# Loading the weights of an FFN layer's first two groups by pairs of tiles, and earlier

## The chip, the cores and the metric

The kernel runs on one core of one Trainium2 chip. The metric is the time of one execution in device microseconds, the median of the runs. A profile is one execution, recorded by the hardware profiler; its times are microseconds from the first instruction (the span's start). TensorE (PE in the profile; PEld for its weight loads) multiplies, VectorE (DVE), ScalarE (ACT) and GpSimd (POOL) work element by element, SyncE (SP) issues most DMA transfers.

## The reference

A two-layer decoder trunk over 512 positions of 1024 channels in float32. Each layer adds a mixer to the residual stream and then a gated FFN:

```python
hn = rms_norm(h, norm_ffn[layer])
g  = causal_dwconv3(hn @ w_gate, conv_w) + conv_b      # 1024 -> 2816
up = hn @ w_up                                         # 1024 -> 2816
h  = h + (jax.nn.silu(g) * up) @ w_down                # 2816 -> 1024
```

`rms_norm` divides by the root of the mean square over the 1024 channels and multiplies by a gain. After layer 1 a final `rms_norm` is applied. The two mixers (gated convolution with pooling in layer 0, spatial gating in layer 1) are not touched by the change.

## The kernel before

**Precision.** Every float32 product is made of three matmuls: an operand is split into a rounded high part and the remainder (`hi` and `lo`), and `mm3` (L135 to L137) adds hi·hi, hi·lo and lo·hi in one PSUM bank. Splitting a weight tile is `parts` (L130, L131): ScalarE rounds `raw` to `whi`, VectorE subtracts to get `wlo`. A matmul of 128x128 weights with 512 positions is one of the 128x512 rows.

**Layout.** The residual stream is held transposed: eight tiles `h[k]` of 128 channels by 512 positions. `hg[k]` holds the split of `h[k]` times the norm's gain. The list `PAIRS` is 0, 4, 1, 5, 2, 6, 3, 7: the order in which the eight channel tiles are multiplied. A "step" below is one entry of `PAIRS`, counted from 0.

**The FFN.** `Ffn.hidden(f)` produces two of the 22 hidden tiles, f and f+1, from a group of weights: 256 columns of the gate and 256 of the up matrix, each loaded in two tiles ("halves") of four channel tiles, 512 KB each. Group f = 0 is multiplied by `direct` before the norm's factor is known, on `hg` with the gain only; the factor `rstd` is applied to the outputs when they leave PSUM (`evacuate`). In step order, each step makes twelve matmuls: two gate and two up outputs, three each. Inside this group two short pieces of TensorE work find the factor: `rstd_tokens` (L211, L212: sums of squares over channels, into columns, with the last tile's square kept apart in `last`), then a short chain on VectorE and ScalarE, then `rstd_spread` (L219: the columns turned into a full tile, copied by ScalarE, L222). Then `normalize(kp)`, four times, makes the normalized `hg` of tiles kp and kp+4 (`x` at L560, the split at L564 and L565) and sums and differences of halves of them (`t`, L572 to L575; L580 to L582 split these, where the low part is made by a copy of the negative and a DMA on GpSimd's queue that adds `t` to it). Group f = 2 is multiplied by `direct` on the normalized tiles, first the gate outputs (48 matmuls), then the up outputs (48). All later groups go through `seven`, which needs the sums too and starts with the `ua` product (L649).

In layer 1, `sums` puts the split of the sums into the buffers of `h[kp]` and `h[kp+4]`, which are free once the residual has been turned: `turn_residual` (L872, four transposes; L874, ScalarE's copy) brings `h` back to positions by channels, half a row of 128 positions each time, eight times in all. Before, one turn stands ahead of each of the eight steps of group 0.

**Buffers.** Weight tiles rotate: four `raw`, five `whi`, five `wlo`. `x` and `t` share three buffers with the tag "sum". TensorE has seven PSUM banks with the tag "mm" and one apart.

**Order of the work.** The engines run their own queues in order. The order within a queue is chosen when the program is built, from the order in which the source issues the operations and from when their inputs and buffers are expected. In the program before, VectorE's `wlo` of group 2's second gate half comes, in layer 0, after all but the last operation of the normalizing, and in layer 1 about half way; the up halves of that group come later still.

Of the kernel before, what the change touches and what calls it, by code (L numbers as in the profile page):

```python
# [8 lines left out]
F32 = mybir.dt.float32  # L9
# [6 lines left out]
P = 128  # L16
# [14 lines left out]
def tile_trunk(ctx: ExitStack, tc: tile.TileContext, x, norm_mix, norm_ffn, final_norm,  # L31
# [3 lines left out]
    nc = tc.nc  # L35
# [4 lines left out]
    wp = ctx.enter_context(tc.tile_pool(name="wp", bufs=1))  # L40
# [86 lines left out]
    def parts(raw, a, b, name):  # L127
        hi = wp.tile([P, a, b], F32R, tag="whi", bufs=5, name=f"whi_{name}")
        lo = wp.tile([P, a, b], F32R, tag="wlo", bufs=5, name=f"wlo_{name}")
        nc.scalar.activation(hi, raw, AF.Copy)  # L130
        nc.vector.tensor_tensor(lo, raw, hi.bitcast(F32), ALU.subtract)  # L131
        return hi, lo

    def mm3(ps, lhs, rhs, start, stop):
        nc.tensor.matmul(ps, lhs[0], rhs[0], start=start, stop=False)  # L135
        nc.tensor.matmul(ps, lhs[0], rhs[1], start=False, stop=False)  # L136
        nc.tensor.matmul(ps, lhs[1], rhs[0], start=False, stop=stop)  # L137
# [27 lines left out]
    def hg_k(k):  # L165
        return hg[k][0], hg[k][1]
# [313 lines left out]
    def ffn_weights(layer, f, order):  # L480
        cs = slice(f * P, (f + 2) * P)
        return {(key, half): fetch(
            (w_ffn_gate if key == "g" else w_ffn_up)[layer][half * 512 : (half + 1) * 512, cs]
            .rearrange("(k p) c -> p k c", p=P), 4, 256, f"{key}{layer}_{f}_{half}")
            for key, half in order}

    class Ffn:
# [27 lines left out]
        def act(self, ft, s):  # L515
            self.acts[ft] = split(self.ap, s, f"a{self.layer}_{ft}", tag="a", bufs=6)

        def direct(self, f, normed, sets, before=lambda i: None):

            layer = self.layer  # L520
            order = [(key, half) for js in sets for half in range(2)
                     for key in dict.fromkeys("gu"[j // 2] for j in js)]
            ch = {key: parts(*raw) for key, raw in ffn_weights(layer, f, order).items()}
            banks = {}
            for js in sets:
                for i, k in enumerate(PAIRS):
                    before(i)
                    for j in js:
                        hi, lo = ch["gu"[j // 2], k // 4]
                        c = slice((j % 2) * P, (j % 2 + 1) * P)  # L530
                        if j not in banks:
                            banks[j] = mm_bank(f"gu{layer}_{f}_{j}")
                        mm3(banks[j], (hi[:, k % 4, c], lo[:, k % 4, c]), hg_k(k),
                            i == 0, i == NK - 1)

            def evacuate():
                r = self.r
                gates = []
                for j in range(2):
                    t = padded_tile()  # L540
                    if normed:
                        nc.scalar.copy(t[:, 2:], banks[j])
                    else:
                        nc.vector.tensor_tensor(t[:, 2:], banks[j], r, ALU.mult)
                    s = self.silu(self.conv(t, f + j), f + j)
                    if not normed:
                        nc.gpsimd.tensor_tensor(s, s, r, ALU.mult)
                    gates.append(s)
                for j, s in enumerate(gates):
                    nc.vector.tensor_tensor(s, banks[2 + j], s, ALU.mult)  # L550
                    self.act(f + j, s)

            return evacuate
# [140 lines left out]
            nc.vector.tensor_tensor(s0, kept[:, :2, :], s0, ALU.mult)  # L694
            self.act(f, s[0])

        def hidden(self, f, before=lambda i: None):
            if f == 0:
                def first(i):
                    before(i)  # L700
                    if i == 2:
                        self.norm.rstd_tokens()
                    elif i == 4:
                        self.r = self.norm.rstd_spread()

                rest = self.direct(0, False, (range(4),), first)
                for kp in range(NP - 1):
                    self.normalize(kp)
                rest()
                self.normalize(NP - 1)  # L710
            elif f == 2:
                self.direct(2, True, ((0, 1), (2, 3)))()
            else:
                self.seven(f)

# [142 lines left out]
    def ffn1(norm):  # L858
        with tc.tile_pool(name="f1", bufs=1) as ap:
            def sums(kp):  # L860
                return [cp.tile([P, 2, HALF], F32R, tag=f"h{k}", name=f"t23_{k}")
                        for k in (kp, kp + NP)]

            ffn = Ffn(1, prm1, norm, ap, sums)
            acts = ffn.acts
            y = [ap.tile([P, D], F32, name=f"y{t}") for t in range(NT)]
            ssf = ap.tile([P, NT, PAD], F32, name="ssf")[:, :, :2]

            def turn_residual(t, half):
                ps = mm_bank(f"hT{t}_{half}")  # L870
                for i in range(4):
                    nc.tensor.transpose(ps[:, i * P : (i + 1) * P],  # L872
                                        h[half * 4 + i][:, t * P : (t + 1) * P], ident)
                nc.scalar.copy(y[t][:, half * 512 : (half + 1) * 512], ps)  # L874

            def before(k):
                if k < 4:
                    turn_residual(k, 0)
                elif k < 8:
                    turn_residual(k - 4, 1)  # L880

            for a, b in PARTS:
                for f in range(a, b, 2):
                    ffn.hidden(f, before=before)
                last = b == NF
                if last:
                    fin = wp.tile([P, D], F32, tag="raw", bufs=4, name="fin")
                    nc.scalar.dma_start(
                        fin, final_norm.rearrange("(o d) -> o d", o=1).to_broadcast([P, D]))
                    root = small[:, 2:3]  # L890
                    nc.scalar.activation(root, eps, AF.Sqrt)
                ch = {}
                for ft in range(a, b):
                    ch[ft] = weights(w_ffn_down[1][ft * P : (ft + 1) * P, :]
                                     .rearrange("(k p) c -> p k c", p=P), 1, D, f"dn1_{ft}")

                def lhs(ft, j):
                    ts_ = slice((j // 2) * P, (j // 2 + 1) * P)
                    return acts[ft][0][:, ts_], acts[ft][1][:, ts_]

                def rhs(ft, j):
                    c = slice((j % 2) * 512, (j % 2 + 1) * 512)
                    return ch[ft][0][:, 0, c], ch[ft][1][:, 0, c]

                yf = {}

                def done(j, ps):
                    t, half = j // 2, j % 2
                    dst = y[t][:, half * 512 : (half + 1) * 512]
                    nc.vector.tensor_tensor(dst, ps, dst, ALU.add)  # L910
                    if not last:
                        return
                    sq = tp.tile([P, S], F32, tag="sq", name=f"sqf{j}")
                    ss = ssf[:, t, half : half + 1]
                    nc.scalar.activation(sq, dst, AF.Square, accum_out=ss)
                    yf[half] = ap.tile([P, S], F32, tag="s", bufs=3, name=f"yf{j}")
                    nc.vector.tensor_tensor(yf[half], dst, fin[:, half * 512 : (half + 1) * 512],
                                            ALU.mult)
                    if half == 0:
                        nc.vector.tensor_scalar(ss, ss, 1.0 / D, EPS, op0=ALU.mult, op1=ALU.add)  # L920
                        return
                    ms = ssf[:, t, 0:1]
                    nc.vector.scalar_tensor_tensor(ms, ss, 1.0 / D, ms, op0=ALU.mult, op1=ALU.add)
                    r = tp.tile([P, LINE], F32, tag="rc", name=f"rc_fin{t}")[:, :1]
                    newton(ms, 1, f"fin{t}", r)
                    nc.vector.tensor_scalar(ms, ms, 1.5, None, op0=ALU.add)
                    for c in range(2):
                        cs = slice(c * 512, (c + 1) * 512)
                        nc.vector.tensor_scalar(y[t][:, cs], yf[c], r, ms,
                                                op0=ALU.mult, op1=ALU.mult)  # L930
                        nc.sync.dma_start(out[t * P : (t + 1) * P, cs], y[t][:, cs])

                group8(f"dn{a}", list(range(a, b)), lhs, rhs, 4, done)
# [47 lines left out]
```

## Time and profile before

| | |
|---|---|
| median of 3 runs | 1031.02 us (1030.04 to 2592.89) |
| profiled execution, its own time | 1031.83 us |
| its span, first to last instruction | 1029.8 us |
| mean granted TensorE clock | 0.991 of full speed |
| TensorE busy | 1004.6 us, 5169 matmuls |
| VectorE, ScalarE, GpSimd busy | 609.5, 471.6, 93.8 us |
| HBM read | 98.42 MB, 98 GB/s over the span |

A row of the order in time has start, duration, engine, line, operation, output<-inputs, sizes and count, and in brackets the idle time of that engine before it with what ended it. A row of waits has engine, output and line, what it waited for, then the total in us, the number of times, and the longest. Matmuls overlap: a row of 0.39 us is followed by the next start 0.23 us later. The granted clock is the share of full speed that TensorE was allowed. A table row by stretches has the stretch, its length, busy time of TensorE, its weight loads, VectorE, ScalarE and GpSimd with numbers of instructions, then the granted clock, the DMA share and GB/s.

### The profile page before, as it was taken

The page shows a single profiled execution, that of the slowest core. Times are in us where ns is not written, and L with a number is a line of the kernel's source. Part 1 is how long each engine was busy: PE and PEld are TensorE (multiplying, and loading weights), DVE is VectorE, ACT ScalarE, POOL GpSimd, SP SyncE. Part 2 cuts the span into 40 slices and gives each one's busy share as a digit, 9 for nine tenths or more (in the row PEclk, how much of TensorE's full clock was granted, in tenths as well). Part 3 has the DMA queues.
Part 4 walks back from the last instruction along what each step waited for, and adds up shares of the span by engine and source line. Part 5 has one row for each costly group of instructions (what it writes and reads, how often), then busy time and mean ns, then how long its engine had stood idle before and what let it go on. Part 6 is the DMA issues. An engine that isn't in the chain of part 4 may idle for free.

```text
span 1029.8 us, 12982 instructions
## 1 busy us (share of the span) xinstructions
PE 1004.6 (98%) x5169; PEld 856.7 (83%) x5169; DVE 609.5 (59%) x878; ACT 471.6 (46%) x689; POOL 93.8 (9%) x105
## 2 busy tenths in 40 slices
PE   9999998899999999999999999989999999999996
PEld 6788886788998899889888888867889988998885
DVE  5997556755556455736843645377645564664566
ACT  5423435551644246326555443476424532660553
POOL 3141122200000000000310001122000000000000
PEclk9999999899999999999999999999999999999998
DMA  7432233442454243524343123245415342543432
GB/s 228 155 102 82 82 115 69 125 146 80 106 140 143 72 127 110 148 78 132 115 142 103 67 96 92 74 82 138 148 56 138 115 143 72 142 118 98 115 91 81
DMA packets 79624, 114.98 MB, mean 112 GB/s; under 512 B 3813, under 2 KB 53197, under 8 KB 79565
## 3 DMA queue, kind: packets, MB, share of 16 engines
q1 hardware_dynamic: 73324, 98.96, 30.7%
q0 software_dynamic: 4896, 13.63, 7.3%
q10 hardware_dynamic: 1344, 1.58, 0.5%
q8 instruction: 40, 0.66, 0.3%
q14 instruction: 20, 0.16, 0.0%
HBM read 98.42 MB, written 2.10 MB: 98 GB/s over the span
## 4 chain that ended last, share of the span: by engine, by line
PE 92%; DVE 4%; DMA 1%; ACT 1%; issue 1%; POOL 0%; SPq 0%; DVEq 0%; ACTq 0%; POOLq 0%
PE ua L649 10%; PE g L136 6%; PE g L135 6%; PE g L137 6%; PE ue L649 5%; PE d L136 4%; PE d L135 4%; PE d L137 4%; PE dn L135 4%; PE dn L136 4%; PE dn L137 4%; PE ub L649 3%; PE gu L137 2%; PE gu L136 2%; PE gu L135 2%; PE v L135 1%
## 5 line engine op out<-in xcount | busy, mean ns | idle before, releaser
L135 PE MATMUL g<-hgh,whi_g 128*128 128x512 f32 x288 | 112.5, 391 | 0.0
L136 PE MATMUL g<-hgl,whi_g 128*128 128x512 f32 x288 | 112.5, 391 | 0.0
L137 PE MATMUL g<-hgh,wlo_g 128*128 128x512 f32 x288 | 112.1, 389 | 0.0
L130 ACT ACTIVATE whi_g<-raw_g 128x1024 fp32r<-128x1024 f32 x44 | 46.4, 1053 | 102.4 <-PE dn L137 57.3
L131 DVE TENSOR_TENSOR wlo_g<-raw_g,whi_g 128x1024 fp32r<-128x1024 f32 x44 | 53.7, 1220 | 29.6 <-ACT whi_g L130 29.6
L135 PE MATMUL dn<-whi_dn,a_hi 128*128 128x512 f32 x176 | 68.5, 389 | 0.0
L136 PE MATMUL d<-a_lo,whi_d 128*128 128x512 f32 x176 | 68.5, 389 | 0.0
L136 PE MATMUL dn<-wlo_dn,a_hi 128*128 128x512 f32 x176 | 68.5, 389 | 0.0
L137 PE MATMUL d<-a_hi,wlo_d 128*128 128x512 f32 x176 | 68.5, 389 | 0.0
L137 PE MATMUL dn<-whi_dn,a_lo 128*128 128x512 f32 x176 | 68.3, 389 | 0.0
L135 PE MATMUL d<-a_hi,whi_d 128*128 128x512 f32 x176 | 68.2, 390 | 0.0
L123 POOL DMA_DIRECT2D wlo_u<-raw_u x18 | 15.4, 855 | 548.4 <-ACT wlo_u L122 232.5
L506 DVE SCALAR_TENSOR_TENSOR c<-rows,prm,c 128x512 f32<-128x512 f32 x88 | 63.5, 746 | 1.2 <-ACT c L504 0.6
L137 PEld LDWEIGHTS g<-hgh,wlo_g 128*128 128x128 f32 x288 | 54.1, 188 | 11.9 <-DVE wlo_g L131 0.5
L135 PEld LDWEIGHTS g<-hgh,whi_g 128*128 128x128 f32 x288 | 54.2, 188 | 10.4
L136 PEld LDWEIGHTS g<-hgl,whi_g 128*128 128x128 f32 x288 | 54.2, 188 | 9.8
L606 DVE TENSOR_TENSOR wlo_a<-raw_u,whi_a 128x512 fp32r<-128x512 f32 x18 | 12.5, 692 | 81.9 <-ACT whi_a L605 81.9
L667 ACT COPY kept<-ua 128x256 f32<-128x256 f32 x54 | 19.8, 367 | 77.3 <-PE ua L649 77.3
L131 DVE TENSOR_TENSOR wlo_d<-raw_d,whi_d 128x1024 fp32r<-128x1024 f32 x22 | 26.8, 1219 | 36.1 <-ACT whi_d L130 36.1
L131 DVE TENSOR_TENSOR wlo_dn<-raw_dn,whi_dn 128x1024 fp32r<-128x1024 f32 x22 | 26.8, 1217 | 35.5 <-ACT whi_dn L130 35.5
L910 DVE TENSOR_TENSOR y<-dn,y 128x512 f32<-128x512 f32 x32 | 22.0, 689 | 42.9 <-PE dn L137 42.9
L605 ACT ACTIVATE whi_s<-s 128x1024 fp32r<-128x1024 f32 x36 | 38.1, 1057 | 16.6 <-PE d L136 14.2
(319 smaller groups left out, 2760.8 us busy)
## 6 DMA issues: line engine op xcount, KB each, us to landing
raw_g<-in_w_ffn_gate_dram SPq DMA_DIRECT2D x44, 512.0 KB
raw_u<-in_w_ffn_up_dram SPq DMA_DIRECT2D x44, 512.0 KB
raw_d<-in_w_ffn_down_dram SPq DMA_DIRECT2D x22, 512.0 KB
raw_dn<-in_w_ffn_down_dram SPq DMA_DIRECT2D x22, 512.0 KB
wlo_u<-raw_u POOLq DMA_DIRECT2D x18, 512.0 KB, 4.6
raw_oe<-in_w_out_even_dram SPq DMA_DIRECT2D x8, 512.0 KB
raw_v<-in_w_in_odd_dram SPq DMA_DIRECT2D x8, 512.0 KB
raw_u<-in_w_in_odd_dram SPq DMA_DIRECT2D x8, 512.0 KB
```

The costliest lines, as they stand in the source:

```text
L123: nc.gpsimd.dma_start(lo, raw, accum_op=ALU.add)
L130: nc.scalar.activation(hi, raw, AF.Copy)
L131: nc.vector.tensor_tensor(lo, raw, hi.bitcast(F32), ALU.subtract)
L135: nc.tensor.matmul(ps, lhs[0], rhs[0], start=start, stop=False)
L136: nc.tensor.matmul(ps, lhs[0], rhs[1], start=False, stop=False)
L137: nc.tensor.matmul(ps, lhs[1], rhs[0], start=False, stop=stop)
L506: nc.vector.scalar_tensor_tensor(c, t[:, i : S + i], prm("cf", i * NF + ft), c, op0=ALU.mult, op1=ALU.add)
L605: nc.scalar.activation(hi, src, AF.Copy)
L606: nc.vector.tensor_tensor(lo, src, hi.bitcast(F32), ALU.subtract)
L649: nc.tensor.matmul(ps, l, r, start=at not in opened, stop=end, skip_group_check=True)
L667: nc.scalar.copy(kept[:, i, :], ps)
L910: nc.vector.tensor_tensor(dst, ps, dst, ALU.add)
```

## The change

The weights of groups 0 and 2 are no longer loaded by halves of channel tiles 0 to 3 and 4 to 7, but so that a half holds the tiles of four successive steps: 0, 4, 1, 5 and 2, 6, 3, 7. Each half comes by two DMAs of 256 KB in place of one of 512. `pair_weights` loads and splits them, and is called for group 2 ahead of the normalizing. The sums of squares move from before step 2 to before step 1, and the spread of the factor from before step 4 to the middle of step 2. In layer 1 the eight turns of the residual stand in steps 0 and 1, one ahead of each output's three matmuls.

```diff
-        def direct(self, f, normed, sets, before=lambda i: None):
+        def pair_weights(self, f, order):
+
+            ch = {}
+            for key, half in order:
+                name = f"{key}{self.layer}_{f}_{half}"
+                raw = wp.tile([P, 4, 2 * P], F32, tag="raw", bufs=4, name=f"raw_{name}")
+                w = (w_ffn_gate if key == "g" else w_ffn_up)[self.layer][:, f * P : (f + 2) * P]
+                w = w.rearrange("(h k p) c -> p h k c", h=2, p=P)
+                for h_ in range(2):
+                    nc.sync.dma_start(raw.rearrange("p (k h) c -> p h k c", h=2)[:, h_],
+                                      w[:, h_, 2 * half : 2 * half + 2])
+                ch[key, half] = parts(raw, 4, 2 * P, name)
+            return ch
+
+        def direct(self, f, normed, sets, ch, before=lambda i, j: None):
...
-            order = [(key, half) for js in sets for half in range(2)
-                     for key in dict.fromkeys("gu"[j // 2] for j in js)]
-            ch = {key: parts(*raw) for key, raw in ffn_weights(layer, f, order).items()}
             banks = {}
             for js in sets:
                 for i, k in enumerate(PAIRS):
-                    before(i)
                     for j in js:
-                        hi, lo = ch["gu"[j // 2], k // 4]
+                        before(i, j)
+                        hi, lo = ch["gu"[j // 2], i // 4]
...
-                        mm3(banks[j], (hi[:, k % 4, c], lo[:, k % 4, c]), hg_k(k),
+                        mm3(banks[j], (hi[:, i % 4, c], lo[:, i % 4, c]), hg_k(k),
                             i == 0, i == NK - 1)
...
-                def first(i):
-                    before(i)
-                    if i == 2:
+                def first(i, j):
+                    before(i, j)
+                    if (i, j) == (1, 0):
                         self.norm.rstd_tokens()
-                    elif i == 4:
+                    elif (i, j) == (2, 2):
                         self.r = self.norm.rstd_spread()
 
-                rest = self.direct(0, False, (range(4),), first)
+                ch = self.pair_weights(0, [("g", 0), ("u", 0), ("g", 1), ("u", 1)])
+                rest = self.direct(0, False, (range(4),), ch, first)
+                self.ch = self.pair_weights(2, [("g", 0), ("g", 1), ("u", 0), ("u", 1)])
                 for kp in range(NP - 1):
                     self.normalize(kp)
                 rest()
                 self.normalize(NP - 1)
             elif f == 2:
-                self.direct(2, True, ((0, 1), (2, 3)))()
+                self.direct(2, True, ((0, 1), (2, 3)), self.ch)()
...
-            def before(k):
-                if k < 4:
-                    turn_residual(k, 0)
-                elif k < 8:
-                    turn_residual(k - 4, 1)
+            def before(i, j):
+                if i < 2:
+                    turn_residual(j, i)
```

In the built program with the change, each engine has as many instructions as before but SyncE, which has sixteen DMA issues more. On ScalarE the high parts of group 2's second gate half and first up half follow the first normalized pair of tiles and precede the first sums' split; on VectorE their low parts stand among the first sums. VectorE's multiplication by the first activation (`s`) of group 0 now precedes the `hgl` of tiles 3 and 7. The transposition of the next layer's parameters (L94) moves on TensorE from group 2 of layer 0 to just ahead of that layer's last down projection.

More of the change, by code (lines that the diff above doesn't have):

```diff
@@ L695, in seven, with hidden @@
             self.act(f, s[0])
-        def hidden(self, f, before=lambda i: None):
+        def hidden(self, f, before=lambda i, j: None):
             if f == 0:
-                def first(i):
-                    before(i)
-                    if i == 2:
+                def first(i, j):
+                    before(i, j)
+                    if (i, j) == (1, 0):
                         self.norm.rstd_tokens()
-                    elif i == 4:
+                    elif (i, j) == (2, 2):
                         self.r = self.norm.rstd_spread()
-                rest = self.direct(0, False, (range(4),), first)
+                ch = self.pair_weights(0, [("g", 0), ("u", 0), ("g", 1), ("u", 1)])
+                rest = self.direct(0, False, (range(4),), ch, first)
+                self.ch = self.pair_weights(2, [("g", 0), ("g", 1), ("u", 0), ("u", 1)])
                 for kp in range(NP - 1):
```

## The prediction

> **What bounds the kernel.** I read the page's engine table first, then the list of what TensorE waited for, then the order in time of TensorE and VectorE around the two places that list names, and last the chain and the granted clock there.
>
> ```profile
> PE 1004.6 (98%) x5169; PEld 856.7 (83%) x5169; DVE 609.5 (59%) x878; ACT 471.6 (46%) x689; POOL 93.8 (9%) x105
> ...
> PE gu L137 <- DVE wlo_g L131: 7.4, 1, 7.4
> PE gu L135 <- ACT hgh L564: 3.7, 1, 3.7
> PE gu L136 <- DVE hgl L565: 1.8, 1, 1.8
> ```
>
> TensorE is busy 98% of the span, so only its waits can be won. All long ones are at `gu`, and in time they lie in group 2 of each FFN: one in layer 0, two in layer 1.
>
> ```profile
> 172.38 0.39 PE L135 MATMUL gu<-hgh,whi_g 128*128 128x512 f32 x1
> ...
> 184.12 1.22 PE L137 MATMUL gu<-hgh,wlo_g 128*128 128x512 f32 x2 [7.42 <-DVE wlo_g L131]
> 185.57 0.63 PE L136 MATMUL gu<-hgl,whi_g 128*128 128x512 f32 x1
> ...
> 204.70 0.28 PE L649 MATMUL ua<-hgh,whi_a 128*128 128x256 f32 x1
> ```
>
> Group 2 starts at 172.38 and hands over to group 4 at 204.70: 32.32 us for 96 matmuls. Undisturbed, twelve take 2.72 us (148.30 to 151.02), 0.2267 each, so 96 take 21.76: layer 0 loses **10.56 us** here. In layer 1 the same stretch is 683.08 to 713.28, 30.20 us with some 0.70 of group 4's work inside: it loses **7.74 us**. Together 18.30 us: that is the ceiling of the change.
>
> Why group 2 waits in layer 0: VectorE's queue.
>
> ```profile
> 162.28 1.41 DVE L560 SCALAR_TENSOR_TENSOR x<-h,prm,rstd_f 128x512 f32<-128x512 f32 x2 [5.46 <-ACT rstd_f L222]
> ...
> 172.92 0.43 DVE L574 TENSOR_TENSOR t<-x 128x256 f32<-128x256 f32 x1 [1.23 <-DMA t<-t]
> ...
> 182.85 1.22 DVE L131 TENSOR_TENSOR wlo_g<-raw_g,whi_g 128x1024 fp32r<-128x1024 f32 x1
> 185.24 0.69 DVE L550 TENSOR_TENSOR s<-gu,s 128x512 f32<-128x512 f32 x1 [1.17 <-POOL s L547]
> ```
>
> Normalizing begins at 162.28, and the low part of group 2's second gate half stands behind all of it, at 182.85. TensorE needs that half in its second step. In layer 1 tile 3's `hg` is late instead: its `x` waits for accumulations (a DMA wait of 3.89 us at 688.52 on VectorE) that in turn wait for `h` buffers.
>
> **Group 0.** The step order is the same in both kernels; only which half a step reads changes. No row shows a wait for group 0's weights, so pairing saves nothing there; what it does is free the first halves' buffers after step 3 rather than step 6. TensorE's set of instructions is unchanged: group 0 still ends at 172.38 and 683.08. The sum of squares is now wanted before step 1, at 151.02; its last square ends at 150.79 (150.17 + 0.62): 0.2 us of cover, and without it a loss of that size. In layer 1 it is wanted at about 660.3 and ready at 657.70.
>
> The sixteen added DMA issues (eight a layer) stand on SyncE's queue. SyncE mostly waits for a buffer. No row gives its cost per issue; the nearest is POOL's 0.86 us, so 0 to 6.9 us a layer on that queue. Below nothing is excluded because both halves of a tile must land before it is split. I take 0: every tile of group 0 was split before TensorE came to it, and the last one is now wanted at step 4.
>
> **rstd.** From 151.02: sums 1.70, step 1 2.86, half of step 2 1.36, so the spread starts near 156.97 instead of 161.03, and VectorE's first `x` moves from 162.28 to 158.2. In layer 1 the eight residual turns (0.48 each on TensorE, the same work as before) now come ahead: 655.22, four turns with step 0 4.64, then 0.48 + 1.70 + step 1 with three turns 4.21, half a step 1.36: spread at 667.61 instead of 670.25, first `x` at 668.92 instead of 671.56. A turn uses one of three free banks; the first that is reused is wanted at 659.2, its copy (0.57, ACT free at 657.60) ends at 658.2. That is 1 us of cover.
>
> **The normalizing, laid out by hand** (layer 0, in the built program's order, with durations from rows: 0.67 for `x` and conv, 0.60 for a 512 subtract, 0.34 for 256, 1.14 for a weight; ACT 0.52 and 0.95). Three weight tiles are now inside it. `whi_g` of the second half needs the buffer of group 0's first gate half; its last reader ends at 160.31, so ACT starts it at 160.4, and the next, whose buffer frees at 161.67, at 161.75. Queued behind both on ACT are the first sums' copies, which start at 163.1 (before: 166.81). VectorE has both low parts by 164.12 and the first `t` complete at 164.46; POOL issues the second accumulation at 165.5.
>
> Now the new wait: the third `x` takes the buffer of the first `t`, so it waits for both accumulations. The chain has
>
> ```profile
> 168.78 4.02 DMA t<-t
> ...
> 682.05 6.03 DMA t<-t
> ```
>
> 4.02 us from issue when alone, 6.03 with a third accumulation and weight traffic beside it. Here two weight loads, freed by the two early low parts, run beside it. Ends: 169.5 and 171.5; I take 170.4, nearer the first because only two accumulations are in flight. Behind this wait in VectorE's queue: 2.68 for `x` and `t`, 0.60 for the first evacuation, 1.20 for `hgl`, 1.14 weight, 0.34: 176.36; then conv, evacuation and `x` alternate, 4.9 us to 181.3. ACT's activation ends at 180.4 and POOL's product follows. That product took 2.4 us with VectorE working (182.77 to 185.24) and 1.25 without; I take 2.4, since VectorE works to 181.3. So the `s` multiply starts at 182.9, and `hgl` of k=3, now queued behind it, is done at 184.2.
>
> TensorE wants that `hgl` after 37 matmuls of group 2, at 180.77. It waits until 184.25: **3.5 us lost** in place of 10.56. Layer 1's hand layout has all of these 510.7 us later, TensorE included (691.24 against 180.54): again **3.5**. There the two waits go because the early residual turns free the `h` buffers that the sums are written to.
>
> **The clock.** In layer 0's gap the granted clock fell to 0.50 and stayed until 188; matmuls were 0.43 apart, some 2 us lost. In layer 1 it stayed at 1.00 through the 3.73 gap and fell only after the 1.83 one:
>
> ```profile
> 698.00:700.00 2.00, 0.48 (x2) 0.44 (x3) 1.83 (x4) 1.39 (x3) 0.14 (x1) 1.00 0.49 172
> 700.00:702.00 2.00, 2.00 (x7) 1.57 (x6) 2.00 (x5) 1.33 (x3) 0.00 (x0) 0.52 0.04 8
> ```
>
> Half clock lasted some 3.4 us, worth 1.7. Two new gaps of 2.9 us idle: nothing to 3.4 us together. I take 2. [...]
>
> **Elsewhere.** The parameter transpose that stood inside layer 0's gap (176.44, 0.26) goes ahead of the last down projection: +0.26. Group 4's weights are split by about 197.7 on VectorE, wanted near 200: 2 us of cover, and no later wait of size exists.
>
> **Sum.** 18.30 − 7.0 − 2.0 − 0.26 = 9.0 us. The profiled execution took 1031.83 (span 1029.8 and 2.0 around it): 1022.8. It lies 0.8 above the median of the runs shown, so I say **1022.0**.
>
> **Rivals.**
> 1. *Accumulations and product are quick.* Landing at 169.5, product 1.25: `hgl` comes 2.1 us earlier, 1.4 lost a layer, no half clock: 18.30 − 2.8 − 0.3 = 15.2, so 1015.8 by the median. For: the 4.02 row. Against: two loads run at that time. 0.17.
> 2. *No half clock, otherwise as laid out:* 1020.0. For: 1.00 through a gap of 3.73 us. Against: the 1.83 gap. 0.15; it lies inside the forecast's own range. [...]
> 3. *The wait moves on to group 4.* VectorE splits the second gate half of group 4 some 5 us later than laid out, so TensorE waits 3 us beyond the cover in both layers: 1022 + 6 = 1028. For: the cover is 2 us and the queue ahead of it long. Against: VectorE is 59% busy, and all its weights' loads now come earlier. 0.14.
> 4. *Slower.* The early weights' loads hold the accumulations, which hold the third `x` and so every later `hgl`. Each us adds one per layer. With half clock in both (3.4) the new loss equals the old 18.30 at 7.3 us per layer, that is when landing is 3.8 us later than I take it: 8.7 us after issue. At 10 us: 2 × 1.3 = 2.6 worse than before, 1033.6. Against: 6.03 is the longest row. 0.07.
> 5. *The change doesn't do what it says* (early parts still end behind the normalizing): excluded by the built order; only the time of buffers could restore it, which is rival 4.
>
> **Numbers.** Forecast 0.47 with its own range 1019 to 1025.5; the rivals as given (0.17, 0.15, 0.14, 0.07). Range 1015.5 to 1028: it leaves out the slower rival and the outer part of the third. Within 2% of 1031.02 means 1010.4 to 1051.6, about what a measurement of this kernel can tell from no change. The ceiling, 18.3, is below 20.6, and no rival adds 20: faster 0.02, same 0.95, slower 0.03.
>
> **What would show it.** Right: no wait of `gu` for `wlo_g`; VectorE's first `x` near 158.2 and 668.9; its third `x` waiting for a DMA until about 170.4 and 681; one TensorE wait of about 3 us per layer, for `hgl`; group 4 starting near 198.5 and 709. Wrong: a wait of TensorE at `g` or `ua`, accumulations over 7 us, or a wait for the sum of squares before step 1.

## The result, and the profile after

The changed kernel takes **1025.79 us**, the median of 5 runs (1025.45 to 1027.54), against 1031.02 for the kernel before. The ratio is 0.9957, with a 95% interval of 0.9941 to 0.9972: it is faster by some 4.4 us (2.9 to 6.1 by the interval), where 9.0 were forecast. (One run of the kernel before, at 2592.89, is far off all others and stands outside the ratio.) The profiled execution took 1027.26 us, its span is 1025.5, against 1031.83 and 1029.8.

From the list of TensorE's waits, of the kernel after:

```profile
PE gu L136 <- DVE hgl L576: 5.5, 2, 2.7
PE gu L135 <- ACT hgh L575: 3.5, 2, 1.9
```

TensorE is as busy as before (1005.2 us, 1004.6 before). Its wait for `wlo_g` (7.4 us) is gone, and so are layer 0's short one for `rows` (0.6) and layer 1's two (3.7 and 1.8). In their place stands one pair of waits in each layer, for the two halves of `hg` of tile 3. In the order in time of TensorE, layer 0:

```profile
172.27 0.39 PE L135 MATMUL gu<-hgh,whi_g 128*128 128x512 f32 x1
...
182.54 0.50 PE L135 MATMUL gu<-hgh,whi_g 128*128 128x512 f32 x1 [1.95 <-ACT hgh L575]
185.77 0.79 PE L136 MATMUL gu<-hgl,whi_g 128*128 128x512 f32 x1 [2.73 <-DVE hgl L576]
...
201.89 0.28 PE L660 MATMUL ua<-hgh,whi_a 128*128 128x256 f32 x1
```

Group 2 starts at 172.27 and group 4 at 201.89: 29.62 us for 96 matmuls that take 21.76 undisturbed, so 7.86 are lost, where it was 10.56. In layer 1 it is 680.40 to 708.40, 28.00: 6.24 lost, where it was 7.74. Together **14.10 in place of 18.30**. That is 4.2 less, and the span is 4.3 shorter: the whole result lies in group 2, as forecast, but less was won there.

The loss has two parts. After 36 matmuls at 0.2267 the first that needs tile 3 was due at 180.43 and started at 182.54; the next was due at 182.77 and started at 185.77: 2.11 + 3.00 = 5.11 us of waiting. The other 2.75 is half clock. In layer 1 the same sums give 4.75 and 1.49. A row of the table by stretches, with the granted clock third from the end:

```profile
186.00:188.00 2.00, 2.00 (x5) 1.59 (x6) 2.00 (x5) 0.72 (x2) 0.00 (x0) 0.50 0.00 0
```

Matmuls follow each other by 0.43 there in place of 0.227. VectorE, in order of time, tells why `hgl` came late:

```profile
158.10 1.42 DVE L571 SCALAR_TENSOR_TENSOR x<-h,prm,rstd_f 128x512 f32<-128x512 f32 x2 [4.09 <-ACT rstd_f L222]
...
171.75 0.75 DVE L571 SCALAR_TENSOR_TENSOR x<-h,prm,rstd_f 128x512 f32<-128x512 f32 x1 [3.88 <-DMA t<-t]
...
179.74 0.74 DVE L571 SCALAR_TENSOR_TENSOR x<-h,prm,rstd_f 128x512 f32<-128x512 f32 x1
...
183.98 0.69 DVE L561 TENSOR_TENSOR s<-gu,s 128x512 f32<-128x512 f32 x1 [1.17 <-POOL s L558]
184.59 1.74 DVE L576 TENSOR_TENSOR hgl<-x,hgh 128x512 fp32r<-128x512 f32 x2
```

The first `x` starts 4.2 us earlier than before. Of this, 3.88 are given back at the third `x`, which waits for the accumulations of tile 0's sums. Tile 3's `x` comes at 179.74, three us later than in the kernel before (176.67), and its `hgl` stands behind the multiplication by `s`, which waits for GpSimd. On ScalarE `hgh` of tile 3 stands behind a table load and an activation. That wait adds no time of its own, since `hgl` comes later still, but it makes two gaps of one.

```profile
179.94 1.28 ACT L512 ACT_TABLE_LOAD   x1
181.24 0.72 ACT L512 ACTIVATE s<-c,prm 128x512 f32<-128x512 f32 x1
181.87 1.13 ACT L575 ACTIVATE hgh<-x 128x512 fp32r<-128x512 f32 x2
```

### The profile page after: what moved, and what is told of

Its sections match the earlier page's. It is cut to its first block, busy times and chain, and to the rows that moved or that the text cites. A ratio compares the mean times of both kernels' runs of the same rounds, so it can differ in the third digit from the quotient of the medians.

```text
span 1025.5 us, 13018 instructions
## 1 busy us (share of the span) xinstructions
PE 1005.2 (98%) x5169; PEld 857.4 (84%) x5169; DVE 611.0 (60%) x878; ACT 472.2 (46%) x689; POOL 91.8 (9%) x105
## 4 chain that ended last, share of the span: by engine, by line
PE 92%; DVE 3%; ACT 2%; DMA 1%; issue 1%; POOL 0%; DVEq 0%; ACTq 0%; POOLq 0%
PE ua L660 10%; PE g L136 6%; PE g L135 6%; PE g L137 6%; PE ue L660 5%; PE d L136 4%; PE d L137 4%; PE d L135 4%; PE dn L136 4%; PE dn L137 4%; PE dn L135 4%; PE ub L660 3%; PE gu L136 2%; PE gu L137 2%; PE gu L135 2%; PE v L135 1%
```

## The experiments

All runs, each with the kernel before measured beside it on the same chip. The loss is that of group 2 in the profiled execution, reckoned as above (start of group 2 to the first `ua`, less 21.76).

| kernel | median us | ratio to before, 95% interval | loss, layers 0 + 1 |
|---|---|---|---|
| before | 1031.0 | 1 | 10.56 + 7.74 |
| after (the whole change) | 1025.79 | 0.9957 [0.9941, 0.9972] | 7.86 + 6.24 |
| rstd_only | 1019.14 | 0.9886 [0.9869, 0.9902] | 3.75 + 1.99 |
| pairs_only | 1016.78 | 0.9868 [0.9853, 0.9883] | 1.44 + 2.68 |
| rest_last | 1015.77 | 0.9857 [0.9843, 0.9872] | 0.42 + 0.24 |
| x2_behind | 1016.27 | 0.9857 [0.9843, 0.9871] | 1.60 + 1.36 |
| light_loads | 1019.96 | 0.9900 [0.9882, 0.9918] | 4.11 + 2.40 |
| warm | 1023.53 | 0.9929 [0.9916, 0.9943] | 5.13 + 4.87 |
| x_own_rest_last | 1012.98 | 0.9832 [0.9817, 0.9847] | 0 + 0 |
| before_x_own_rest_last | 1027.83 | 0.9972 [0.9962, 0.9982] | 9.03 + 7.12 |
| best_late_turns | 1013.74 | 0.9835 [0.9821, 0.9848] | 0 + 0 |
| best_late_rstd | 1012.78 | 0.9824 [0.9811, 0.9838] | 0 + 0 |
| best_halves0 | 1012.13 | 0.9818 [0.9805, 0.9832] | 0 + 0 |
| best_rstd_only | 1013.96 | 0.9836 [0.9822, 0.9849] | 0.75 + 0.76 |

A span less its loss is 1010 to 1013 us in every one of these profiles. What is outside group 2 differs by up to 3 us, so the column of losses explains the column of times down to that size, and not below. (The kernel before is 1031 in each of the three comparisons: 1030.72, 1031.35, 1031.04. Its loss in layer 1 is less 0.70 for work of group 4 done inside.)

### Each part alone: rstd_only

```diff
 # before.py, with the change's positions of rstd and turns, not its weights
+                    if (i, j) == (1, 0):
                         self.norm.rstd_tokens()
+                    elif (i, j) == (2, 2):
                         self.r = self.norm.rstd_spread()
...
+            def before(i, j):
+                if i < 2:
+                    turn_residual(j, i)
```

> One part alone: the kernel before, with only the sums of squares, the spread and the residual turns moved to the first steps; all weights by halves of channel tiles, group 2's issued after the normalizing. Theory A (the loss is set by where hgl of tile 3 stands in VectorE's queue and by when its x may start; early weights are not what wins): first x at 158.2 and about 669; in this built order the low part of group 2's second gate half stands ahead of tile 3's x, and hgl of tile 3 ahead of the multiplication by s. By the shifted rows of the kernel before, hgl of tile 3 ends near 179.2, before TensorE wants it (180.6); the second up half's low part is late by 2 to 3 us in each layer, so 5 to 8 us lost of the 18.3: 1018 to 1021, faster than the whole change. Theory B (the early weights make the gain): the wait for wlo_g stays, only shifted by 4.1 and 2.6 us: 1025 to 1028, not faster than the whole change.

Measured 1019.14: theory A. VectorE in layer 0, in order of time:

```profile
165.07 1.42 DVE L560 SCALAR_TENSOR_TENSOR x<-h,prm,rstd_f 128x512 f32<-128x512 f32 x2
167.72 0.43 DVE L574 TENSOR_TENSOR t<-x 128x256 f32<-128x256 f32 x1 [1.23 <-DMA t<-t]
...
169.94 1.22 DVE L131 TENSOR_TENSOR wlo_g<-raw_g,whi_g 128x1024 fp32r<-128x1024 f32 x1
...
176.58 1.29 DVE L565 TENSOR_TENSOR hgl<-x,hgh 128x512 fp32r<-128x512 f32 x2
```

`hgl` of tile 3 is done at 177.87, before TensorE wants it (37 matmuls after 171.20, 179.6). The third `x` does not wait here: it starts as tile 1's last `hgl` ends (164.35 + 0.69), and in the built program it has the address of tile 1's `x`. The first sum made from it takes the buffer with the DMA and waits, but only 1.23 us, since the second accumulation lands 4.1 us after its issue (163.58 to 167.7). What is left is the late up half, as expected:

```profile
PE gu L137 <- DVE wlo_u L131: 3.5, 2, 1.8
```

**Less than the whole change is worth more than the whole change**: the early weights, added to this, cost 6.6 us by the medians.

### The other part alone: pairs_only

```diff
 # after.py, with rstd and turns at their old steps
-                    if (i, j) == (1, 0):
+                    if (i, j) == (2, 0):
                         self.norm.rstd_tokens()
-                    elif (i, j) == (2, 2):
+                    elif (i, j) == (4, 0):
...
-                if i < 2:
-                    turn_residual(j, i)
+                if j == 0:
+                    turn_residual(i % 4, i // 4)
```

> The other part alone: weights of groups 0 and 2 by pairs and issued ahead of the normalizing, as in the change; sums of squares, spread and residual turns at their old steps. Theory A: first x at 162.3 as before; no wait for wlo_g, but hgl of tile 3 stands behind the multiplication by s and comes at about 187 in layer 0, where TensorE waits some 6 us and half clock follows; in layer 1 the sums' split waits for the late residual turns, loss as before, 7 to 8: together 15 to 17 of 18.3 lost, 1028 to 1031. Theory B: most of the gain of 5 stays: 1025 to 1027.

Measured 1016.78. **Both expectations failed**, theory A's most (1028 to 1031). VectorE, layer 0:

```profile
160.04 1.23 DVE L131 TENSOR_TENSOR wlo_g<-raw_g,whi_g 128x1024 fp32r<-128x1024 f32 x1 [3.91 <-ACT whi_g L130]
161.41 1.23 DVE L131 TENSOR_TENSOR wlo_u<-raw_u,whi_u 128x1024 fp32r<-128x1024 f32 x1
162.55 1.41 DVE L571 SCALAR_TENSOR_TENSOR x<-h,prm,rstd_f 128x512 f32<-128x512 f32 x2
...
171.02 1.41 DVE L571 SCALAR_TENSOR_TENSOR x<-h,prm,rstd_f 128x512 f32<-128x512 f32 x2
...
181.81 0.69 DVE L561 TENSOR_TENSOR s<-gu,s 128x512 f32<-128x512 f32 x1 [1.18 <-POOL s L558]
...
183.08 0.68 DVE L576 TENSOR_TENSOR hgl<-x,hgh 128x512 fp32r<-128x512 f32 x1
```

I had shifted the rows of the kernel after by the later first `x`. But here VectorE splits the two weight tiles in the idle time ahead of the first `x`, the two loads that this sets free run ahead of the first accumulations (issued at 168.00 and 169.03), and the third `x`, at 171.02, waits for nothing. In the built program it has the address of tile 1's `x` here too, and not that of the first `t`, which the accumulation issued at 169.03 still reads. In the kernel after it has that of the first `t`. The table by stretches (DMA share and GB/s are the last two columns), first of the kernel after, then of pairs_only:

```profile
164.00:166.00 2.00, 2.00 (x11) 1.65 (x10) 2.00 (x5) 1.69 (x5) 1.55 (x2) 1.00 0.88 255
166.00:168.00 2.00, 2.00 (x11) 1.65 (x10) 1.87 (x4) 0.66 (x3) 0.18 (x1) 1.00 1.02 207
168.00:170.00 2.00, 2.00 (x10) 1.66 (x9) 0.00 (x0) 1.06 (x2) 0.86 (x1) 1.00 1.10 261
```

```profile
162.00:164.00 2.00, 2.00 (x11) 1.65 (x10) 2.00 (x4) 0.65 (x2) 0.00 (x0) 1.00 0.74 189
164.00:166.00 2.00, 2.00 (x10) 1.67 (x9) 2.00 (x5) 0.62 (x1) 0.00 (x0) 1.00 0.81 235
166.00:168.00 2.00, 2.00 (x10) 1.67 (x9) 2.00 (x5) 1.47 (x3) 0.00 (x0) 1.00 0.32 112
```

In the kernel after the DMA share is 0.88 to 1.10 while its accumulations (issued at 163.85 and 165.31) run; in pairs_only the loads are through before (0.32 from 166 to 168). `hgl` of tile 3 does stand behind `s`, as expected, but it comes 1.5 us earlier than in the kernel after, although the normalizing began 4.45 us later. Layer 1, with its turns at the old steps, loses 2.68, not the 7 to 8 that I put on late turns.

So theory A in its first form (only the order and the start of `x`) was too narrow. What the two halves of the change do to each other begins with the wait at the third `x`.

### The order alone: rest_last and x2_behind

```diff
 # rest_last: after.py, group 0's evacuation after the last normalize
-                for kp in range(NP - 1):
+                for kp in range(NP):
                     self.normalize(kp)
                 rest()
-                self.normalize(NP - 1)
 # x2_behind: after.py, one pin
+                if kp == 2:
+                    inorder(ins)
```

> The change with one edit: the evacuation of group 0 (conv, activation, product) is issued after the fourth normalize call in place of before it, so that x and hgl of tile 3 stand ahead of most of conv, of the table load, the activation and the multiplication by s. Theory A: the fourth x then waits for the accumulations of tile 1's sums (issued 168.8 and 173.8, landing near 178), hgl of tile 3 is done near 181.5, TensorE waits 0.5 to 1.5 us in each layer and the clock stays up: loss per layer from 7.6 and 5.8 to 1 to 1.5, so 1015 to 1018. Rival C (the gap is set by the landing of the accumulations alone, the order costs nothing): 1023 to 1026.

> The change with one pin: the x of tile 2 may not pass the last sum of tile 1 on VectorE. It still takes the buffer of the first sums and still waits for their accumulations (about 3.7 us, until about 171.7 and 679.5). But the built order that follows has both hgl of tile 3 ahead of the multiplication by s, and ScalarE's two hgh of tile 3 ahead of the table load. If that order is what costs (theory A): hgl of tile 3 ends near 181.7 and 689.5 in place of 185.7 and 693.5, TensorE waits 0.5 to 1.7 us per layer, no half clock: 1014 to 1018, with the 3.9 us wait of VectorE unchanged. If the wait for the accumulations is what costs, wherever hgl stands (rival C): 1024 to 1026.

Measured 1015.77 and 1016.27, both as theory A has it; rival C falls. x2_behind, VectorE in layer 0:

```profile
171.76 1.42 DVE L571 SCALAR_TENSOR_TENSOR x<-h,prm,rstd_f 128x512 f32<-128x512 f32 x2 [3.38 <-DMA t<-t]
...
181.40 0.69 DVE L578 TENSOR_TENSOR hgl<-x,hgh 128x512 fp32r<-128x512 f32 x1
...
184.88 0.69 DVE L561 TENSOR_TENSOR s<-gu,s 128x512 f32<-128x512 f32 x1 [1.19 <-POOL s L558]
```

The third `x` starts at 171.76, to 0.01 us where the kernel after has it, and still waits 3.38 for the same accumulations. But tile 3's `x` starts 1.65 earlier in this order (178.09), its `hgl` runs at 181.40 and not at 184.59, ScalarE's `hgh` is ahead of the table load, and TensorE waits 1.26 and 1.06 us in all, with the clock at 1.00 throughout. Group 2 loses 2.96 us in place of 14.10: some 3.5 us of waiting less in each layer, and all of the half clock. The medians are 9.5 apart. In rest_last group 2 loses next to nothing, and a small wait, for `wlo_g`, moves on to group 4: 0.77 and 0.76 us (rival 3 of the prediction, at a quarter of its size).

So neither thing alone loses much: with the wait at the third `x`, but `hgl` ahead of `s`, group 2 loses 2.96 (x2_behind); with `hgl` behind `s`, but no such wait, 4.12 (pairs_only). The kernel after has both, and loses 14.10.

### The landing alone: light_loads

```diff
 # after.py; the loads are cut, all compute instructions stay
         if f == 4:
...
+                n = 1 if (key, half) in (("u", 1), ("g", 0)) else 4
+                nc.sync.dma_start(raw[:, :n, :], src[:, :n, :])
...
+                    raws[kh] = (r[:, 0:1, :].to_broadcast([P, 4, 2 * P]), *rest)
```

> The change with the two weight loads that run beside the first accumulations cut to a quarter: of group 4's second up half and first gate half only the first channel tile is loaded (128 KB in place of 512), and it stands for all four in the split and in the products, so the output is another; the instructions of all compute engines are the same, in the same order. If the collision with these loads makes the landing late: the second accumulation lands 4.0 to 4.6 us after issue in place of 6.4, the third x starts at 169.4 to 170.0 in place of 171.75, hgl of tile 3 comes some 2 us earlier, TensorE's two gaps together are 2 to 3 us per layer in place of 4.7 and 4.3, and half clock may stay or go: 1017 to 1022. If the landing is late for another reason (two accumulations at once): the third x stays at 171.5 or later and the time at 1025 to 1026.5.

Measured 1019.96, inside the first expectation. VectorE, layer 0:

```profile
168.90 0.75 DVE L581 SCALAR_TENSOR_TENSOR x<-h,prm,rstd_f 128x512 f32<-128x512 f32 x1 [1.08 <-DMA t<-t]
...
181.76 1.74 DVE L586 TENSOR_TENSOR hgl<-x,hgh 128x512 fp32r<-128x512 f32 x2
```

The second accumulation is issued at 165.25 and the third `x` starts at 168.90, 3.65 us later, where the kernel after needs 6.35 from issue to landing (165.31 to 171.66). So the collision with the weight loads is what makes the landing late. The wait at tile 3 falls from 5.11 to 2.33, by 2.78 for a third `x` 2.85 earlier: one us per us, as the prediction's fourth rival had it. How the accumulations and the loads share the DMA engines, no run here shows.

### The clock alone: warm

```diff
 # after.py; ahead of tile 3's first product eight matmuls into a spare bank, behind it eleven
+                            for n in range(8):
+                                inorder(nc.tensor.matmul(warm, hg[0][0][:, :P], hg[0][0],
+                                                         start=n == 0, stop=n == 7))
```

> The change with TensorE's gaps filled: ahead of the first product of tile 3 in group 2 eight matmuls of 128x512 into a spare bank, and eleven behind it, ahead of the one that waits for hgl (1.8 and 2.5 us, into gaps of 1.95 and 2.73); they add nothing to the output. The data come no earlier, so group 2's wait for hgl stays until about 185.8 and 693.5. If half clock after the gaps costs what I read (2.9 us in layer 0, 1.4 in layer 1): granted clock 1.0 there, 1021 to 1022.5. If it costs the 2.0 in all that the prediction took: 1023.5 to 1024.5. If filling brings nothing: 1025 to 1026.5.

Measured 1023.53, which by time alone fits the smaller price (the 2.0 of the prediction). The trace says otherwise. TensorE, layer 0:

```profile
180.16 1.97 PE L547 MATMUL warm<-hgh 128*128 128x512 f32 x8
182.39 2.68 PE L552 MATMUL warm<-hgh 128*128 128x512 f32 x11
...
185.34 0.50 PE L554 MATMUL gu<-hgl,whi_g 128*128 128x512 f32 x1 [0.27 <-DVE hgl L591]
```

Matmuls follow each other by 0.227 to 0.24 behind the second gap in both layers' group 2, where it was 0.43 in the kernel after, so half clock is gone there (the mean granted clock of the execution is 0.997 in place of 0.993), and the loss is 5.13 and 4.87: within 0.12 the waiting of the kernel after (5.11, 4.75), without its 2.75 and 1.49. So half clock costs 4.1 us in group 2. Only 2.3 arrive in the median time. In this profile most of the difference is a wait in layer 1's mixer, outside the change, which the kernel after doesn't show; why it comes was not tried.

```profile
PE wst L777 <- POOL ws L770: 1.6, 1, 1.6
```

### Neither the wait nor the order: x_own_rest_last, and the same edits without the change

```diff
 # after.py, and in the second kernel before.py; with rest_last's edit
-            x = self.ap.tile([P, 2, S], F32, tag="sum", bufs=3, name=f"x{n}")
+            x = [self.ap.tile([P, S], F32, tag=f"a{p}", bufs=6, name=f"x{p}{n}")
+                 for p in ("hi", "lo")]
```

> The change with two edits: the evacuation after the fourth normalize call, and x in two tiles of the activations' buffers (idle then) in place of the buffers it shares with the sums, so that no x waits for an accumulation. Theory A: no wait of 3.9 and 3.5 us on VectorE before the third x, hgl of tile 3 done near 174, no TensorE wait in group 2 in either layer, no half clock there: nearly the whole ceiling is won, 1012 to 1014. Rival D (the wait moves on to group 4, whose splits and group 0's evacuation now stand behind): a wait of 1 to 3 us per layer at ua or g, 1015 to 1019.

> The kernel before with the two edits that brought the changed kernel to 1013 (x in the activations' buffers, group 0's evacuation issued after the fourth normalize call), and nothing of the change. If the change is needed for that time (theory A): the low part of group 2's second gate half still stands behind all the normalizing, at about 181 in layer 0, where TensorE waits some 5 us, and in layer 1 some 3 to 4 us; with half clock 1022 to 1027. If the two edits do it alone (rival E): 1012 to 1015.

With the change: 1012.98, the whole ceiling. VectorE, layer 0:

```profile
166.72 0.75 DVE L572 SCALAR_TENSOR_TENSOR xhi<-h,prm,rstd_f 128x512 f32<-128x512 f32 x1
...
173.39 0.69 DVE L577 TENSOR_TENSOR hgl<-xhi,hgh 128x512 fp32r<-128x512 f32 x1
...
175.00 0.69 DVE L577 TENSOR_TENSOR hgl<-xlo,hgh 128x512 fp32r<-128x512 f32 x1
```

Here `xhi` is the `x` of the first tile of a pair and `xlo` that of the second. `hgl` of tile 3 is done at 174.08 and that of tile 7 at 175.69, both over 5 us before they are wanted (179.6 and 181.0), and TensorE waits for nothing in group 2 or 4 in either layer; rival D falls. Without the change: 1027.83, a little above the 1022 to 1027 expected, and rival E falls. `wlo_g` is what TensorE waits for again:

```profile
PE gu L137 <- DVE wlo_g L131: 6.1, 2, 5.0
PE gu L135 <- ACT whi_u L130: 3.4, 1, 3.4
```

So with these two edits beside it the change is worth 14.9 us (1027.83 to 1012.98), some three times what it showed.

### What of the change is needed once x is free

All four start from edits shown above. best_late_turns and best_late_rstd are x_own_rest_last with the turns, or the turns, sums of squares and spread, as in pairs_only. best_rstd_only is rstd_only with the two edits of x_own_rest_last. best_halves0 is x_own_rest_last with group 0's weights by halves again (`direct` then picks group 0's half by the channel tile, not shown here):

```diff
-                ch = self.pair_weights(0, [("g", 0), ("u", 0), ("g", 1), ("u", 1)])
+                ch = {kh: parts(*raw) for kh, raw in ffn_weights(
+                    self.layer, 0, [("g", 0), ("u", 0), ("g", 1), ("u", 1)]).items()}
```

> The 1013 us kernel (the change, x in the activations' buffers, group 0's evacuation last) with the residual turns of layer 1 back at one per step. The prediction held that the early turns take away layer 1's waits by freeing the buffers of h. With no x waiting for an accumulation, a later split of the sums should not reach TensorE: 1012 to 1014.5. If the early turns are needed: a wait in layer 1 for hgl or at ua of 2 us or more, 1015 to 1018.

> The 1013 us kernel with the whole second part of the change undone: sums of squares, spread and turns at their old steps; only pairs of tiles and the early issue stay. VectorE then does two low parts before the first x (162.5) and has about 16.6 us of work up to hgl of tile 3: 179.1, TensorE wants it at 180.6. If the early rstd only buys slack: 1012 to 1014.5. If it is needed: hgl late by 2 us or more per layer, 1016 to 1020.

> The 1013 us kernel with group 0's weights by halves of channel tiles as before; group 2's stay by pairs and are issued ahead of the normalizing, rstd and turns stay early. The buffer for group 2's second gate half comes free at about 167.1 in place of 160.3, its low part is done near 170 and with pairs TensorE wants it only in group 2's fifth step, near 176.7. If pairing group 0 buys only slack: 1012 to 1014.5. If it is needed: a wait for wlo_g or hgl of 2 us or more per layer, 1016 to 1020.

> The kernel before with the early rstd and turns, x in the activations' buffers and the evacuation last; no pairs, no early issue. The low part of group 2's second gate half again stands behind the normalizing, at about 176, and without pairs TensorE wants it in the second step, near 172.6 (some up products may go ahead of it). If the first part of the change is what wins once no x waits: 2 to 5 us lost per layer, 1017 to 1023. If it is not: 1012 to 1014.5.

Measured 1013.74, 1012.78, 1012.13 and 1013.96: all in the range for parts that buy only slack. In the fourth, where the early weights are gone, the 1017 to 1023 given for the case that they are what wins did not come. There the low part of the second gate half comes at 174.30, as I had it within 2 us, but in this built order TensorE does eight other matmuls ahead of the first that needs it, and waits for `wlo_g` for 0.8 us in all.

Beside the two edits either part of the change alone is enough: with early weights the normalizing may start late, and with an early start the weights may come late. Without both it is 1027.83. Which of the kernels at 1012 to 1014 is best, these intervals don't tell; all of them beat the kernel before and the kernel after.

## Why the prediction was wrong, step by step

The mechanism was right, and two terms of the sum were too small: the waiting (7.0 taken, 9.86 measured) and the half clock (2.0 taken, 4.24 measured). That is why 4.4 us were won and not 9.0.

**Right.** The bound and the ceiling: the span moved as group 2's loss did, to 0.1 us. The first `x` (158.2 forecast, 158.10 measured). No wait for group 0's weights, none for the sum of squares. The accumulations' issue (165.5, 165.31), and that the third `x` would wait for them. That `hgl` of tile 3, behind the multiplication by `s`, would be the new bound. Group 4 in time; added issues on SyncE at nothing.

**Wrong in size: the landing.** I took 170.4 between 169.5 and 171.5 "nearer the first because only two accumulations are in flight". It was 171.66, and relative to TensorE layer 1 was 1.1 late too. The number of accumulations was the wrong criterion: light_loads, with the same two accumulations and less weight traffic, has 3.65 us from issue in place of 6.35. The row to go by was the 6.03, which had weight traffic beside it. Waiting became 5.11 and 4.75 in place of 3.5 and 3.5: **2.9 us**, of which some 2.4 are the landing, at one us per us as in light_loads.

**Wrong in size: the clock.** 2.0 taken, 4.24 measured (warm: 4.10): **2.2 us**. I allowed for 0 to 3.4, from two gaps of 2.9 us idle. But there were two gaps in each layer with a single matmul between them, and the trace's clock record shows half speed for 6.83 us in layer 0, 3.41 in layer 1. That TensorE would also wait for `hgh`, which ScalarE makes behind a table load and an activation, was not in my layout: of ScalarE's queue I took only the time of the activation, and not the place of `hgh`. In layer 0 of the kernel before half speed lasted 10.24 us. What of a gap decides whether half speed follows was not shown: rstd_only has one gap of 1.81 us in layer 0 and some 3.4 us at half speed after it; x2_behind has gaps of 1.26 and 1.06 us and none.

The two errors add to 5.1. Against them stands the 0.26 for the parameter transpose, which lies outside group 2 and which no run shows by itself: 5.1 − 0.26 = 4.8, the difference between the forecast 9.0 and the 4.2 that group 2 gained.

**Not needed: the early turns.** "There the two waits go because the early residual turns free the `h` buffers": pairs_only has the turns at their old steps and loses 2.68 in layer 1 in place of 7.74, and best_late_turns loses nothing. The change with late turns and nothing else was not tried.

**Not seen: that each part is worth more alone.** I summed the change against the kernel before, never its two halves against each other. By the ratios rstd alone brings 12 us, pairs alone 14, both together 4.4. Together, the early low parts free two weight buffers (loads issued at 162.55 and 164.02) just when the accumulations are issued (163.85 and 165.31); the third `x` takes the buffer of the first `t`, which these still read, not tile 1's `x` buffer as in either half; and `hgl` lands behind `s`. The third rival (group 4) didn't come; the fourth had the right law, one us per us of landing, at a smaller lateness. The time, 1025.79, is inside the range but just above the likeliest case's own (1019 to 1025.5).

Why the planner gives the third `x` one buffer in the one program and another in the next was not tried.

## What to carry to other kernels

Before crediting a step that starts earlier, find the first instruction behind it that takes a buffer which a DMA still reads, and price that DMA with the traffic that the same change sets free. Then look where the bound's last input stands on every engine that makes it: behind an activation and a GpSimd product it costs their time (in the kernel after 1.28 us for the table load, 0.72 for the activation and 1.91 for the product), and one pin of order was worth 9.5 us here. Test the parts of a change one by one: two edits that bring 12 and 14 us may bring 4.4 together.

## What the runs showed of the hardware that was not expected

- A 256 KB accumulating DMA had landed 3.65 us after its issue with two 128 KB loads beside it (light_loads), and 6.35 us after it with two 512 KB loads (after). In rstd_only, with no weight load but two more accumulations issued before it landed, it was 4.1.
- A gap of 1.81 us on TensorE was followed by some 3.4 us at half clock, which cost 1.7 us (rstd_only, layer 0); one of 1.66 us in the same execution (layer 1) and one of 2.10 us (light_loads, layer 1) were not followed by any. So the length of a gap alone did not decide; what does was not tried.
